# Hybrid retention and attention block: the opening stage of a one-core kernel, divided anew between VectorE and ScalarE

## Chip, cores and metric

One core of a Trainium2 chip runs one launch of the program. The metric is device time in microseconds of that launch, lower is better, given as the median of several runs on the chip.

## What is computed

One encoder layer on 1024 tokens of 1024 features, all in float32. Cut to the part around the change:

```python
mod = jax.nn.silu(c) @ w_ada + b_ada
shift, scale, gate = jnp.split(mod, 3, axis=-1)
h = rms_norm(x, norm_w) * (1.0 + scale[:, None, :]) + shift[:, None, :]
proj = h @ w_in                      # q, k, v, gate columns of retention; latents and gate of attention
...                                  # retention (4 groups of 2 heads), latent attention (8 heads)
y = jnp.concatenate([ret_out, mla_out], axis=-1) @ w_out
x = x + gate[:, None, :] * y
```

Every product `a @ b` is made of three TensorE products of rounded parts (`mm3`, lines 64 to 67): each operand is split into a high part, a cast to fp32r, and a low part, the difference, and high x high, high x low and low x high are summed in PSUM.

## The kernel before

The work is laid out in stages that follow each other on TensorE: the opening; four retention groups with their gates; two gate pieces of the attention; latents; output projection of the retention half; up-projections; attention over eight heads; output projection of the attention half. Features lie on the partitions: `xn` holds the normalised input as eight blocks `k` of 128 features by 1024 tokens, and `hh[k]`, `hl[k]` are the high and the low part of the modulated features.

**The opening** makes `hh` and `hl` and, beside it, the products of the first retention group. Its helpers are:

- `load` (line 134) issues the loads on SyncE's queue: `x` tiles of 128 tokens (512 KB each), rows of `w_ada` for the scale (`s`) and the shift (`b`) of feature block k, and pages `w` of the first group's weights (two feature blocks a page, two buffers).
- `x_tile(t, bank)` (line 148): sum of squares of a token tile on ScalarE, mean on VectorE, the power -1/2 on GpSimd (`r_x`, line 153), the scaling on VectorE or, for the tiles in `XACT`, on ScalarE (lines 155, 157), eight 128x128 transposes on TensorE, and two copies back into `xn` (ScalarE line 164, VectorE line 166).
- `modulation(k)` (line 173): two sums of 1024 products with `silu(c)`; the first on VectorE (line 176), the second on VectorE for k < `KV0` = 2 (line 179) and else as a product on GpSimd (line 182) and a sum on ScalarE (line 183). They give the column pair `b1` (lines 185, 187).
- `features(k, half)` (line 190): scale and shift on VectorE (line 192), the cast to `hh` on ScalarE (194), the difference `hl` on VectorE (195), each for 512 tokens.
- `w_page(j)` (line 200) calls `split`: cast on ScalarE (line 80), difference `wl` on GpSimd (line 81).
- `products(k, lo, hi)` (line 204): three products of 512 columns for each token tile of a half, into eight PSUM banks that stay open over all k: 24 a block, 192 in all.

All eight token tiles are loaded and transposed first, then k runs from 0 to 7 and both halves of the tokens are done for each. The decay masks (24 small GpSimd instructions, lines 269 to 271, with `Exp` on ScalarE) and the rotary tables (VectorE lines 284 to 314, two `Sin` on ScalarE) are made in the same stretch. The opening ends where the first retention gate's product can take a PSUM bank, which the rotary products (lines 352, 354) have to have read: the row of TensorE at 95.81 us.

The program gives the order in which the code issues things, and a scheduler of the framework reorders the instructions within each engine before the run; on the chip every engine then takes its own queue in order, and waits at each instruction for what it needs. `tc.issue_after` keeps the masks behind a named instruction.

Of the kernel before, what the change touches and what calls it, by code (L numbers as in the profile page):

```python
# [30 lines left out]
def body(tc, I, O):  # L31
# [116 lines left out]
    def x_tile(t, bank):  # L148
        """one token tile: its norm, and its features to the partitions"""
        x_ = ld["x", t]  # L150
        i0 = A.activation(xn[:, :, ts_(t)], x_.rearrange("p (a b) -> p a b", b=P), AF.Square, accum_out=msq[:, t:t + 1])
        V.tensor_scalar(out=msq[:, t:t + 1], in0=msq[:, t:t + 1], scalar1=1.0 / D, scalar2=EPS, op0=ALU.mult, op1=ALU.add)
        i1 = G.tensor_tensor(out=r_x[:, t:t + 1], in0=msq[:, t:t + 1], in1=neghalf[:, 0:1], op=ALU.pow)
        if t in XACT:
            A.activation(x_, x_, AF.Copy, scale=r_x[:, t:t + 1])
        else:
            V.tensor_scalar(out=x_, in0=x_, scalar1=r_x[:, t:t + 1], scalar2=None, op0=ALU.mult)
# [9 lines left out]
        return i0, i1  # L167
# [41 lines left out]
    load(*tuple(("x", t) for t in range(8)))  # L209
    nxt = [("s", 0), ("b", 0), ("w", 0), ("s", 1), ("b", 1), ("s", 2), ("b", 2), ("w", 1), ("s", 3), ("b", 3)]  # L210
    nxt = [a for a in nxt if a not in tuple(("x", t) for t in range(8))]
    for t in range(NT):
        x_last = x_tile(t, acc if t % 2 else sm)
        load(nxt.pop(0))
    load(*nxt)
    acc0 += [acc() for _ in range(4)] + [sm() for _ in range(NB0 - 4)]
    for k in range(KT):
        modulation(k)
        if 4 <= k + 3 < KT:
            load(("s", k + 3), ("b", k + 3))  # L220
        if k % 2 == 0:
            w_page(k // 2)
            if 4 <= k + 2 < 8:
                load(("w", k // 2 + 1))
# [739 lines left out]
```

## Time and profile before

| | |
|---|---|
| runs of the kernel before | 1068.68, 1069.62, 1070.6 us (median 1069.62) |
| span of the profiled execution | 1068.5 us (first to last instruction; its time with what lies around the span is not listed apart) |
| busy in the span | TensorE 1020.6, VectorE 592.4, GpSimd 444.0, ScalarE 427.0 us |
| mean granted TensorE clock | 0.986 |
| first 30 us | VectorE 20.08, ScalarE 22.57, GpSimd 13.84, TensorE 17.85 us busy |
| 30 to 60 us | VectorE 30.00, ScalarE 13.55, GpSimd 25.62, TensorE 21.83 us busy |
| 96 us to the end (972.5 us) | TensorE 953.92 us busy |

The span runs from the first to the last instruction. A row of a timeline gives start, duration, engine, line, operation, output <- input, and in brackets how long the engine stood idle before and what ended it. DVE is VectorE, ACT ScalarE, POOL GpSimd, PE TensorE, SP SyncE, PEclk the granted share of TensorE's clock (1 is 2.4 GHz, 0.5 is 1.2 GHz).

### The profile page before, as it was taken

To read this page: it belongs to the slowest core of one execution; us is meant where nothing else is said; L and a number is where in the kernel's file an instruction comes from. 1 tells how busy PE (TensorE), PEld (TensorE's weight loads), DVE (VectorE), ACT (ScalarE), POOL (GpSimd) and SP (SyncE) were. 2 spreads that over 40 slices of the span, in tenths; PEclk is the share of its full clock that TensorE was granted. 3 is DMA by queue.
4 is the path that set the end of the run, shared out by engine and by line. 5 is a ranking of instruction groups with operands and counts; after the bars stand their busy time and mean duration, and the time that the engine had idled before them with its cause. 6 is when DMAs were issued, how large, how long until landed. Compare 5 with 4: busy or idle time off the path is not lost.

```text
span 1068.5 us, 15240 instructions
## 1 busy us (share of the span) xinstructions
PE 1020.6 (96%) x5736; PEld 889.8 (83%) x5736; DVE 592.4 (55%) x1367; ACT 427.0 (40%) x804; POOL 444.0 (42%) x345
## 2 busy tenths in 40 slices
PE   5669999999999999999999999989999999999998
PEld 5457887888888888898888889879999999888887
DVE  6998645544545444335402114867777878874332
ACT  7526312221321322123423005566777776872100
POOL 3877303221421421115534224953465555863210
PEclk8889999999999999999999999999999999999999
DMA  9513101110210201314444730100000000003432
GB/s 373 189 59 113 46 1 60 60 40 21 99 40 21 84 27 62 117 34 177 149 152 147 235 110 21 40 1 1 21 21 2 21 21 21 20 21 118 156 110 69
DMA packets 30744, 82.27 MB, mean 77 GB/s; under 512 B 3536, under 2 KB 4560, under 8 KB 30672
## 3 DMA queue, kind: packets, MB, share of 16 engines
q1 hardware_dynamic: 25920, 72.92, 20.1%
q10 hardware_dynamic: 4752, 8.39, 2.2%
q8 instruction: 45, 0.74, 0.3%
q14 instruction: 27, 0.22, 0.1%
HBM read 64.52 MB, written 16.78 MB: 76 GB/s over the span
## 4 chain that ended last, share of the span: by engine, by line
PE 84%; DVE 10%; DMA 2%; ACT 2%; issue 1%; POOL 1%; ACTq 0%; DVEq 0%; POOLq 0%
PE acc L67 13%; PE acc L66 13%; PE acc L65 13%; PE pt L737 5%; PE sp L65 4%; PE sp L67 4%; PE sp L66 4%; PE po L66 3%; PE po L67 3%; PE po L65 3%; DMA wa<-w_ada 2%; PE sm L66 2%; PE sm L65 2%; PE sm L67 2%; PE sm L423 2%; PE sm L422 2%
## 5 line engine op out<-in xcount | busy, mean ns | idle before, releaser
L81 POOL TENSOR_TENSOR wl<-wr,wh 128x1024 fp32r<-128x1024 f32 (+2 forms) x55 | 124.7, 2275 | 153.0 <-ACT wh L80 139.6
L67 PE MATMUL acc<-wh,hl 128*128 128x512 f32 (+2 forms) x352 | 128.3, 370 | 5.6 <-DVE hl L195 5.5
L65 PE MATMUL acc<-wh,hh 128*128 128x512 f32 (+2 forms) x352 | 128.9, 366 | 1.3 <-ACT xn L164 0.9
L66 PE MATMUL acc<-wl,hh 128*128 128x512 f32 (+2 forms) x352 | 129.3, 367 | 0.0
L723 POOL TENSOR_SCALAR pr<-pr,st 128x1024 f32<-128x1024 f32 x62 | 72.2, 1168 | 100.9 <-DVE st L722 77.6
L740 DVE TENSOR_TENSOR pl<-pt,ph 128x512 fp32r<-128x512 f32 x128 | 85.7, 683 | 31.3 <-ACT ph L739 31.3
L65 PE MATMUL acc<-hh,wh 128*128 128x512 f32 x256 | 101.0, 395 | 1.7 <-DVE t L354 1.7
L66 PE MATMUL acc<-hl,wh 128*128 128x512 f32 x256 | 100.8, 394 | 0.0
L67 PE MATMUL acc<-hh,wl 128*128 128x512 f32 x256 | 100.8, 394 | 0.0
L80 ACT CAST wh<-wr 128x1024 fp32r<-128x1024 f32 (+2 forms) x55 | 53.7, 980 | 106.3 <-PE sm L66 36.7
L739 ACT CAST ph<-pt 128x512 fp32r<-128x512 f32 x128 | 73.3, 590 | 27.4 <-PE pt L737 25.4
L67 PEld LDWEIGHTS acc<-wh,hl 128*128 128x128 f32 x352 | 66.5, 190 | 14.9 <-DVE hl L195 6.7
L721 ACT ACTIVATE pr<-sp,st 128x1024 f32<-128x1024 f32 x62 | 69.6, 1122 | 23.0 <-DVE st L719 22.9
L66 PE MATMUL po<-pl,vh 128*128 128x256 f32 x256 | 76.4, 298 | 2.1 <-DVE pl L740 2.0
L718 DVE TENSOR_REDUCE st<-sp 128x1 f32<-128x1024 f32 x62 | 75.4, 1216 | 4.1 <-PE sp L67 4.0
L65 PEld LDWEIGHTS acc<-wh,hh 128*128 128x128 f32 x352 | 66.3, 188 | 10.7 <-ACT xn L164 1.2
L66 PEld LDWEIGHTS acc<-wl,hh 128*128 128x128 f32 x352 | 66.4, 189 | 9.0 <-POOL wl L81 0.3
L65 PE MATMUL po<-ph,vh 128*128 128x256 f32 x256 | 73.7, 288 | 0.0
L67 PE MATMUL po<-ph,vl 128*128 128x256 f32 x256 | 72.9, 285 | 0.0
L737 PE MATMUL pt<-ident,pr 128*128 128x128 f32 x496 | 69.8, 272 | 2.9 <-DVE st L722 2.7
L358 POOL TENSOR_TENSOR rb<-t,t 128x128 f32<-128x128 f32 x32 | 14.8, 463 | 133.5 <-PE sm L368 66.8
L737 PEld LDWEIGHTS pt<-ident,pr 128*128 128x128 f32 x496 | 57.8, 140 | 7.5 <-issue 2.9
(359 smaller groups left out, 2524.8 us busy)
## 6 DMA issues: line engine op xcount, KB each, us to landing
x<-w_ada SPq DMA_DIRECT2D x16, 512.0 KB, 7.0
wr<-w_ret SPq DMA_DIRECT2D x16, 512.0 KB, 3.5
wr<-w_rg SPq DMA_DIRECT2D x8, 512.0 KB, 3.4
retD<-ro SPq DMA_DIRECT2D x16, 256.0 KB, 2.1
wr<-w_mg SPq DMA_DIRECT2D x8, 512.0 KB, 3.5
wa<-w_ada SPq DMA_DIRECT2D x8, 512.0 KB, 3.5
wr<-w_out SPq DMA_DIRECT2D x8, 512.0 KB, 4.5
wro<-retD SPq DMA_DIRECT2D x8, 512.0 KB, 4.1
```

Source lines behind the costliest of these rows:

```text
L65: T.matmul(out, lh, rh, start=first, stop=False, **kw)
L66: T.matmul(out, lh, rl, start=False, stop=False, **kw)
L67: T.matmul(out, ll, rh, start=False, stop=last, **kw)
L80: A.copy(out=hi, in_=raw)
L81: G.tensor_tensor(out=lo, in0=raw, in1=hi, op=ALU.subtract)
L422: T.matmul(op[:, ts_(h)], sT[t][:, h], vv[t][:, h], start=True, stop=False)
L718: V.tensor_reduce(out=st_[:, 0:1], in_=sp, op=ALU.max, axis=AX.X)
L721: A.activation(pr, sp, AF.Exp, bias=st_[:, 1:2], scale=sc_, accum_out=st_[:, 2:3])
L723: G.tensor_scalar(out=pr, in0=pr, scalar1=st_[:, 3:4], scalar2=0.0, op0=ALU.mult, op1=ALU.add)
L737: T.transpose(tp[:, ts_(q)], pr[:, ts_(half * 4 + q)], ident)
L739: A.copy(out=ph[half][:, :, c_], in_=tv)
L740: V.tensor_tensor(out=pl[half][:, :, c_], in0=tv, in1=ph[half][:, :, c_], op=ALU.subtract)
```

## The change

In the opening, GpSimd keeps `r_x` alone. The second modulation sum of k = 2 to 7 goes from GpSimd and ScalarE to VectorE; the differences `wl` of the first group's four weight pages and the mask terms go from GpSimd to VectorE (three small GpSimd instructions a head become two on VectorE); the scale and shift of the features (16 instructions) goes from VectorE to ScalarE as one `Identity` activation with per-partition scale and bias; two of the eight sums of squares (tiles 3 and 6) go from ScalarE to VectorE, and the three scalings that ScalarE had go to VectorE. The loads are issued for the first four token tiles, then what feature block 0 needs, then the other four tiles; the first half's features and products of block 0 come before tiles 4 to 7. The rotary temporary `rtmp` moves to the ring of weight buffers, and the two `Sin` come behind a named instruction. The pages of later groups are split as before, `wl` on GpSimd.

```diff
-    def split(raw, shape, tag_h="wh", tag_l="wl", pool=None):
+    def split(raw, shape, tag_h="wh", tag_l="wl", pool=None, eng=G):
...
-        G.tensor_tensor(out=lo, in0=raw, in1=hi, op=ALU.subtract)
+        eng.tensor_tensor(out=lo, in0=raw, in1=hi, op=ALU.subtract)
...
-        i0 = A.activation(xn[:, :, ts_(t)], x_.rearrange("p (a b) -> p a b", b=P), AF.Square, accum_out=msq[:, t:t + 1])
+        if t in XDVE:
+            V.scalar_tensor_tensor(out=xn[:, :, ts_(t)], in0=x_.rearrange("p (a b) -> p a b", b=P), scalar=1.0,
+                                   in1=x_.rearrange("p (a b) -> p a b", b=P), op0=ALU.mult, op1=ALU.mult,
+                                   accum_out=msq[:, t:t + 1])
+        else:
+            A.activation(xn[:, :, ts_(t)], x_.rearrange("p (a b) -> p a b", b=P), AF.Square, accum_out=msq[:, t:t + 1])
...
-        if t in XACT:
-            A.activation(x_, x_, AF.Copy, scale=r_x[:, t:t + 1])
-        else:
-            V.tensor_scalar(out=x_, in0=x_, scalar1=r_x[:, t:t + 1], scalar2=None, op0=ALU.mult)
+        V.tensor_scalar(out=x_, in0=x_, scalar1=r_x[:, t:t + 1], scalar2=None, op0=ALU.mult)
...
-        V.scalar_tensor_tensor(out=wa_s, in0=wa_s, scalar=1.0, in1=sc, op0=ALU.mult, op1=ALU.mult,
-                               accum_out=mp[:, 0:1])
-        if k < KV0:
-            V.scalar_tensor_tensor(out=wa_b, in0=wa_b, scalar=1.0, in1=sc, op0=ALU.mult, op1=ALU.mult,
-                                   accum_out=mp[:, 1:2])
-        else:
-            G.tensor_tensor(out=wa_b, in0=wa_b, in1=sc, op=ALU.mult)
-            A.activation(wa_b, wa_b, AF.Copy, accum_out=mp[:, 1:2])
+        for i, kind in enumerate("sb"):
+            wa = ld[kind, k]
+            V.scalar_tensor_tensor(out=wa, in0=wa, scalar=1.0, in1=sc, op0=ALU.mult, op1=ALU.mult,
+                                   accum_out=mp[:, i:i + 1])
...
-        V.tensor_scalar(out=xn[:, k, sl], in0=xn[:, k, sl], scalar1=b1s[k][:, 0:1], scalar2=b1s[k][:, 1:2],
-                        op0=ALU.mult, op1=ALU.add)
+        A.activation(xn[:, k, sl], xn[:, k, sl], AF.Identity, bias=b1s[k][:, 1:2], scale=b1s[k][:, 0:1])
...
-        w0.append(split(ld["w", j], (("p (k n) -> p k n",), {"k": 2})))
+        w0.append(split(ld["w", j], (("p (k n) -> p k n",), {"k": 2}), eng=V))
...
+    rtmp = p_ring.tile([P, 4, NT, 32], F32, name="rtmp", tag="wh")
+    load(*(("x", t) for t in range(4)), ("s", 0), ("b", 0), ("w", 0), *(("x", t) for t in range(4, 8)))
+    for t in range(4):
+        x_tile(t, acc)
+    load(("s", 1), ("b", 1), ("s", 2), ("b", 2))
+    acc0 += [acc() for _ in range(4)]
+    modulation(0)
+    w_page(0)
+    features(0, 0)
+    products(0, 0, 4)
+    for t in range(4, 8):
+        x_tile(t, sm)
+    acc0 += [sm() for _ in range(4)]
     for k in range(KT):
-        modulation(k)
...
+        if k:
+            modulation(k)
...
-        G.tensor_scalar(out=mt, in0=rel[:, 1], scalar1=lg[:, 8 + h:9 + h], scalar2=0.0, op0=ALU.mult, op1=ALU.add)
-        G.tensor_scalar(out=m2, in0=rel[:, 0], scalar1=lg[:, h:h + 1], scalar2=0.0, op0=ALU.mult, op1=ALU.add)
-        G.tensor_tensor(out=mt, in0=mt, in1=m2, op=ALU.add)
+        V.tensor_scalar(out=m2, in0=rel[:, 1], scalar1=lg[:, 8 + h:9 + h], scalar2=None, op0=ALU.mult)
+        V.scalar_tensor_tensor(out=mt, in0=rel[:, 0], scalar=lg[:, h:h + 1], in1=m2, op0=ALU.mult, op1=ALU.add)
...
-XACT, KACT = (3, 5, 7), 1
+XDVE, KACT = (3, 6), 1
```

What the built programs then hold, at three places. First SyncE's queue at the start; `x<-x` and `xl<-x` are token tiles, `x<-w_ada` modulation rows, `wr<-w_ret` weight pages. Before:

```order
L43 DMA small<-small 128x567
L145 DMA x<-x 128x1024 x6
L145 DMA xl<-x 128x1024 x2
L145 DMA x<-w_ada 128x1024 x2
L145 DMA wr<-w_ret 128x1024 x2
L145 DMA x<-w_ada 128x1024 x8
L145 DMA wr<-w_ret 128x1024
L145 DMA x<-w_ada 128x1024 x2
L145 DMA wr<-w_ret 128x1024
L145 DMA x<-w_ada 128x1024 x4
```

In the change:

```order
L43 DMA small<-small 128x567
L145 DMA x<-x 128x1024 x4
L145 DMA x<-w_ada 128x1024 x2
L145 DMA wr<-w_ret 128x1024
L145 DMA x<-x 128x1024 x2
L145 DMA xl<-x 128x1024 x2
L145 DMA wr<-w_ret 128x1024
L145 DMA x<-w_ada 128x1024 x5
L145 DMA wr<-w_ret 128x1024
L145 DMA x<-w_ada 128x1024
L145 DMA wr<-w_ret 128x1024
L145 DMA x<-w_ada 128x1024 x8
```

The modulation rows of feature block 0 and the first weight page moved ahead of the last four token tiles. The third page now comes after five further modulation rows, before after eight; the fourth has eight rows behind it, before four (they follow the part shown).

Second, GpSimd from the `r_x` on (`mt`, `m` are mask terms, `x<-x,sc` the second modulation product). Before, a part:

```order
L153 TENSOR_TENSOR r_x<-msq,neghalf 128x1 x8
L269 TENSOR_SCALAR mt<-small,lg 128x128
L270 TENSOR_SCALAR m_674<-small,lg 128x128
L269 TENSOR_SCALAR mt<-small,lg 128x128
L271 TENSOR_TENSOR mt<-mt,m_674 128x128
L270 TENSOR_SCALAR m_681<-small,lg 128x128
L271 TENSOR_TENSOR mt<-mt,m_681 128x128
L81 TENSOR_TENSOR wl<-wr,wh 128x1024
L270 TENSOR_SCALAR m_688<-small,lg 128x128
L81 TENSOR_TENSOR wl<-wr,wh 128x1024
L182 TENSOR_TENSOR x<-x,sc 128x1024 x2
```

In the change, all up to the first rotary instruction:

```order
L158 TENSOR_TENSOR r_x<-msq,neghalf 128x1 x8
L81 TENSOR_TENSOR wl<-wr,wh 128x1024 x4
L328 MEMSET rb_750 128x512
L328 MEMSET rb_751 128x512
L81 TENSOR_TENSOR wl<-wr,wh 128x1024 x2
```

Only `r_x` and the six differences of later pages (two of the first gate, four of the second group) are left there.

Third, VectorE where the feature blocks 2 and 3 are made (`hl` of blocks 2 and 3, `rtmp` the rotary table, `b` the column pairs). Before:

```order
L176 SCALAR_TENSOR_TENSOR x,mp<-x,sc 128x1024
L288 TENSOR_SCALAR rtmp<-rtmp 128x256
L195 TENSOR_TENSOR hl_94<-xn,hh_86 128x512
L303 COPY rtmp<-rtmp 128x256
L195 TENSOR_TENSOR hl_94<-xn,hh_86 128x512
L185 SCALAR_TENSOR_TENSOR b_518<-mp,small,c_125 128x1
L289 TENSOR_SCALAR rtmp<-rtmp 128x256
L187 TENSOR_TENSOR b_471<-mp,small 128x1
L195 TENSOR_TENSOR hl_95<-xn,hh_87 128x512
L288 TENSOR_SCALAR rtmp<-rtmp 128x256
L195 TENSOR_TENSOR hl_95<-xn,hh_87 128x512
L192 TENSOR_SCALAR xn<-xn,b_471 128x512 x2
```

In the change:

```order
L178 SCALAR_TENSOR_TENSOR x,mp<-x,sc 128x1024
L181 SCALAR_TENSOR_TENSOR b_465<-mp,small,c_125 128x1
L190 TENSOR_TENSOR hl_94<-xn,hh_86 128x512
L178 SCALAR_TENSOR_TENSOR x,mp<-x,sc 128x1024
L190 TENSOR_TENSOR hl_94<-xn,hh_86 128x512
L178 SCALAR_TENSOR_TENSOR x,mp<-x,sc 128x1024
L183 TENSOR_TENSOR b_465<-mp,small 128x1
L270 TENSOR_SCALAR m_687<-small,lg 128x128
L190 TENSOR_TENSOR hl_95<-xn,hh_87 128x512 x2
L181 SCALAR_TENSOR_TENSOR b_511<-mp,small,c_125 128x1
L288 TENSOR_SCALAR rtmp<-rtmp 128x256
L183 TENSOR_TENSOR b_511<-mp,small 128x1
```

The scale-and-shift row (`xn<-xn,b`) is gone from VectorE, and the sums `x,mp<-x,sc` now stand two for each block between the differences.

## Rows read from the trace of the kernel before

**Rows 1.** The page's part 4: the chain of waits, shares of the span by engine.

```profile
PE 84%; DVE 10%; DMA 2%; ACT 2%; issue 1%; POOL 1%; ACTq 0%; DVEq 0%; POOLq 0%
```

**Rows 2.** Windows: start:end, length, busy us (instructions) per engine, PEclk, DMA share, GB/s.

```profile
0.00:30.00 30.00, 17.85 (x88) 15.14 (x89) 20.08 (x64) 22.57 (x39) 13.84 (x23) 0.89 0.94 364
30.00:60.00 30.00, 21.83 (x80) 16.05 (x79) 30.00 (x38) 13.55 (x30) 25.62 (x17) 0.89 0.45 154
...
96.00:1068.50 972.50, 953.92 (x5464) 837.33 (x5463) 509.11 (x1219) 374.60 (x708) 380.99 (x291) 0.99 0.20 66
```

**Rows 3.** Timeline of TensorE: start us, us, instruction, idle before it and its releaser.

```profile
26.23 0.50 PE L65 MATMUL acc<-wh,hh 128*128 128x512 f32 x1 [0.28 <-ACT hh L194]
...
77.61 0.39 PE L65 MATMUL acc<-wh,hh 128*128 128x512 f32 x1
...
80.33 0.39 PE L65 MATMUL sm<-wh,hh 128*128 128x512 f32 x1
...
95.81 0.47 PE L65 MATMUL acc<-hh,wh 128*128 128x512 f32 x1 [1.72 <-DVE t L354]
```

**Rows 4.** Groups of instructions by form, 0 to 96 us, VectorE: busy us, mean ns.

```profile
L195 DVE TENSOR_TENSOR hl<-xn,hh 128x512 fp32r<-128x512 f32 x16 | 21.5, 1350 | 0.4 <-ACT hh L194 0.4
...
L192 DVE TENSOR_SCALAR xn<-xn,b 128x512 f32<-128x512 f32 x16 | 12.8, 832 | 0.0
...
L176 DVE SCALAR_TENSOR_TENSOR x<-x,sc 128x1024 f32<-128x1024 f32 x8 | 12.2, 1522 | 0.0
...
L289 DVE TENSOR_SCALAR rtmp<-rtmp 128x256 f32<-128x256 f32 x3 | 5.1, 1691 | 0.0
...
L288 DVE TENSOR_SCALAR rtmp<-rtmp 128x256 f32<-128x256 f32 x3 | 3.1, 1048 | 0.0
...
L179 DVE SCALAR_TENSOR_TENSOR x<-x,sc 128x1024 f32<-128x1024 f32 x2 | 4.3, 2130 | 0.0
...
L185 DVE SCALAR_TENSOR_TENSOR b<-mp,small,c 128x1 f32<-128x1 f32 x8 | 4.1, 515 | 0.0
...
L157 DVE TENSOR_SCALAR x<-x,r_x 128x1024 f32<-128x1024 f32 x4 | 3.0, 754 | 0.7 <-POOL r_x L153 0.5
```

**Rows 5.** The same view: GpSimd.

```profile
L81 POOL TENSOR_TENSOR wl<-wr,wh 128x1024 fp32r<-128x1024 f32 x9 | 23.8, 2643 | 12.4 <-ACT wh L80 12.4
...
L182 POOL TENSOR_TENSOR x<-x,sc 128x1024 f32<-128x1024 f32 x6 | 16.6, 2770 | 0.0
...
L271 POOL TENSOR_TENSOR mt<-mt,m 128x128 f32<-128x128 f32 x8 | 4.9, 610 | 0.2
```

**Rows 6.** Timeline of VectorE: single instructions, alone or beside GpSimd.

```profile
22.89 0.55 DVE L192 TENSOR_SCALAR xn<-xn,b 128x512 f32<-128x512 f32 x1
...
26.21 2.48 DVE L195 TENSOR_TENSOR hl<-xn,hh 128x512 fp32r<-128x512 f32 x1 [0.42 <-ACT hh L194]
...
28.61 1.21 DVE L176 SCALAR_TENSOR_TENSOR x<-x,sc 128x1024 f32<-128x1024 f32 x1
...
39.27 0.68 DVE L195 TENSOR_TENSOR hl<-xn,hh 128x512 fp32r<-128x512 f32 x1
...
85.58 0.28 DVE L288 TENSOR_SCALAR rtmp<-rtmp 128x256 f32<-128x256 f32 x1
...
93.02 1.99 DVE L274 TENSOR_SCALAR mask<-mask 128x1024 f32<-128x1024 f32 x1 [2.58 <-ACT mask L272]
```

**Rows 7.** Timeline of GpSimd: single instructions.

```profile
9.07 0.56 POOL L153 TENSOR_TENSOR r_x<-msq,neghalf 128x1 f32<-128x1 f32 x1 [1.01 <-DVE msq L152]
...
24.35 0.46 POOL L271 TENSOR_TENSOR mt<-mt,m 128x128 f32<-128x128 f32 x1
...
25.78 2.37 POOL L81 TENSOR_TENSOR wl<-wr,wh 128x1024 fp32r<-128x1024 f32 x1
```

**Rows 8.** Timeline of ScalarE: the nearest rows to the new feature instruction.

```profile
13.40 1.15 ACT L155 ACTIVATE x<-x,r_x 128x1024 f32<-128x1024 f32 x1
...
25.56 0.62 ACT L194 CAST hh<-xn 128x512 fp32r<-128x512 f32 x1
```

More of the change, by code (lines that the diff above doesn't have):

```diff
@@ L150, in x_tile @@
         x_ = ld["x", t]
-        i0 = A.activation(xn[:, :, ts_(t)], x_.rearrange("p (a b) -> p a b", b=P), AF.Square, accum_out=msq[:, t:t + 1])
-        V.tensor_scalar(out=msq[:, t:t + 1], in0=msq[:, t:t + 1], scalar1=1.0 / D, scalar2=EPS, op0=ALU.mult, op1=ALU.add)
-        i1 = G.tensor_tensor(out=r_x[:, t:t + 1], in0=msq[:, t:t + 1], in1=neghalf[:, 0:1], op=ALU.pow)
-        if t in XACT:
-            A.activation(x_, x_, AF.Copy, scale=r_x[:, t:t + 1])
-        else:
-            V.tensor_scalar(out=x_, in0=x_, scalar1=r_x[:, t:t + 1], scalar2=None, op0=ALU.mult)
+        if t in XDVE:
[4 more added lines that the diff above has]
+            A.activation(xn[:, :, ts_(t)], x_.rearrange("p (a b) -> p a b", b=P), AF.Square, accum_out=msq[:, t:t + 1])
+        V.tensor_scalar(out=msq[:, t:t + 1], in0=msq[:, t:t + 1], scalar1=1.0 / D, scalar2=EPS, op0=ALU.mult, op1=ALU.add)
+        G.tensor_tensor(out=r_x[:, t:t + 1], in0=msq[:, t:t + 1], in1=neghalf[:, 0:1], op=ALU.pow)
+        V.tensor_scalar(out=x_, in0=x_, scalar1=r_x[:, t:t + 1], scalar2=None, op0=ALU.mult)
         for z in range(2):
@@ L166, in x_tile @@
                 V.tensor_copy(out=dst, in_=src)
-        return i0, i1
     b1s = {}
@@ L173, in modulation @@
     def modulation(k):
-        wa_s, wa_b = ld["s", k], ld["b", k]
         mp = p_st.tile([P, 2], F32, name="mp", tag="mp", bufs=3)
-        V.scalar_tensor_tensor(out=wa_s, in0=wa_s, scalar=1.0, in1=sc, op0=ALU.mult, op1=ALU.mult,
-                               accum_out=mp[:, 0:1])
-        if k < KV0:
-            V.scalar_tensor_tensor(out=wa_b, in0=wa_b, scalar=1.0, in1=sc, op0=ALU.mult, op1=ALU.mult,
-                                   accum_out=mp[:, 1:2])
-        else:
-            G.tensor_tensor(out=wa_b, in0=wa_b, in1=sc, op=ALU.mult)
-            A.activation(wa_b, wa_b, AF.Copy, accum_out=mp[:, 1:2])
+        for i, kind in enumerate("sb"):
+            wa = ld[kind, k]
+            V.scalar_tensor_tensor(out=wa, in0=wa, scalar=1.0, in1=sc, op0=ALU.mult, op1=ALU.mult,
+                                   accum_out=mp[:, i:i + 1])
         b1 = p_st.tile([P, 2], F32, name="b1", tag="b1", bufs=3)
@@ L207, in products @@
             mm3(acc0[t], hh[k][:, ts_(t)], hl[k][:, ts_(t)], wh[:, k % 2], wl[:, k % 2], k == 0, k == KT - 1)
[L209 to L216, printed above, removed]
-    for k in range(KT):
-        modulation(k)
-        if 4 <= k + 3 < KT:
-            load(("s", k + 3), ("b", k + 3))
-        if k % 2 == 0:
+    rtmp = p_ring.tile([P, 4, NT, 32], F32, name="rtmp", tag="wh")
[11 more added lines that the diff above has]
+    acc0 += [sm() for _ in range(4)]
+    for k in range(KT):
+        if k:
+            modulation(k)
+        if k % 2 == 0 and k + 2 < KT:
+            load(("w", k // 2 + 1))
+        if 3 <= k + 2 < KT:
+            load(("s", k + 2), ("b", k + 2))
+        if k and k % 2 == 0:
             w_page(k // 2)
-            if 4 <= k + 2 < 8:
-                load(("w", k // 2 + 1))
         for half in range(2):
-            i0 = features(k, half)
+            if k or half:
+                i0 = features(k, half)
+                products(k, 4 * half, 4 * half + 4)
             if k == KACT:
-                x_last = i0, x_last[1]
-            products(k, 4 * half, min(4 * half + 4, NB0))
+                x_last = i0
     lg = ctile("lg", 16)
@@ L262, in body @@
     after = ExitStack()
-    for i_ in x_last:
-        after.enter_context(tc.issue_after(i_.ins))
+    after.enter_context(tc.issue_after(x_last.ins))
     for h in range(H):
@@ L280, in body @@
     V.tensor_copy(out=posf, in_=pos_i)
-    rtmp = p_st.tile([P, 4, NT, 32], F32, name="rtmp", tag="xw", bufs=XW)
     ang, nn, nh, yy = (rtmp[:, j] for j in range(4))
@@ L311, in body @@
     V.tensor_scalar(out=yy, in0=yy, scalar1=PI_IN, scalar2=-PI_IN, op0=ALU.min, op1=ALU.max)
+    after = tc.issue_after(x_last.ins)
+    after.__enter__()
     A.activation(Sr, yy, AF.Sin)
@@ L315, in body @@
     A.activation(Cr, nn, AF.Sin)
+    after.__exit__(None, None, None)
     st.close()
@@ L888 @@
 PREP_0 = (2, 4, 5, 6, 6)
-NB0, NACC, XW, KV0 = 8, 4, 8, 2
+NB0, NACC, XW = 8, 4, 8
 WLX = (6, 7)
-XACT, KACT = (3, 5, 7), 1
+XDVE, KACT = (3, 6), 1
 MG0 = 2
```

## Prediction, made before the changed kernel ran

> **What bounds the kernel now.** I read the chain of waits first: 84% of it is TensorE and 10% VectorE [rows 1]. The windows then say where the two lie. From 96 us on TensorE is busy 953.92 of 972.5 us; in the first 60 us it has 17.85 and 21.83 us in windows of 30, while VectorE has no gap at all from 30 to 60 us [rows 2]. So the opening is VectorE's, the rest is TensorE's, and an opening that ends d earlier should end the program d earlier. Its end is one row: the first product of the retention gate, at 95.81 us, after 1.72 us of waiting for VectorE's rotary products [rows 3].
>
> TensorE alone would need far less for the opening: twelve products go by from 77.61 to 80.33 us, 0.227 us each [rows 3], so the 192 are 43.6 us. VectorE is full, but not all with work. The same `hl` difference of 512 columns takes 0.68 us at 39.27 and 2.48 us at 26.21 us [rows 6]; the second stands beside GpSimd's difference from 25.78 to 28.15 us [rows 7] and ends half a microsecond after it. I read that as VectorE waiting for GpSimd to finish and then doing its 0.6 us.
>
> **What VectorE loses to GpSimd.** Busy time of a group less its count times the row that stands alone [rows 4, 6]: `hl` 21.5 - 16 x 0.68 = 10.6; scale and shift 12.8 - 16 x 0.55 = 4.0; first sums 12.2 - 8 x 1.21 = 2.5; second sums 4.3 - 2 x 1.21 = 1.9; the two rotary roundings 5.1 - 3 x 0.28 = 4.3 and 3.1 - 3 x 0.28 = 2.3; column pairs 4.1 - 8 x 0.28 = 1.9; the mask's scaling 1.99 [rows 6] against 0.75 for a scaling of the same width [rows 4], 1.2. Sum **28.7 us**. GpSimd's work in that stretch, at its single rows [rows 7] times the counts: 9 differences and 6 products [rows 5] at 2.37 are 35.6, 24 mask terms at 0.46 (eight each of three kinds; one kind stands in [rows 5]) 11.0, eight `r_x` at 0.56 4.5, together 51.0 us. VectorE loses 0.56 us for each of them.
>
> **The change, part by part.**
> GpSimd keeps the eight `r_x` and, before the first gate product, five differences of later pages: 4.5 + 11.9 = 16.3 us, which at 0.56 cost VectorE 9.2. It gets back 28.7 - 9.2 = **19.5 us**.
>
> VectorE's own list grows. Six second sums at 1.21 are 7.3; four page differences of 1024 columns, of which no row stands alone here, lie between the sum of that width (1.21) and twice the `hl` row (1.36), I take 1.21 as the row of their own width, 4.8; sixteen mask instructions of 128 columns are at most the 0.28 of a 256-wide row, 4.5; two sums of squares 2.4; three scalings at 0.75 2.3; and the 16 scale-and-shift rows leave, -8.8. That is 12.5, and since a record reaches 0.08 us into the next (2.48 from 26.21 ends at 28.69, the next begins at 28.61 [rows 6]), 15 more records are 1.2 us less: **+11.3 us**.
>
> Loads. In the first 30 us VectorE is idle for 9.9 us and the DMA moves 364 GB/s [rows 2], 1.44 us for 512 KB. Block 0's two rows and page come ahead of four token tiles, so 5.8 us sooner, and two sums and a page difference, 3.6 us, can stand in that idle time: **-3.6** (ends 0 and -5.8, no more than the loads come sooner). The four tiles come 3 x 1.44 = 4.3 us later; what hides it is this same work, and TensorE's first twelve products (2.7 us) on the first half. If that cover fails, those 3.6 are gone.
>
> The other pages: the third and the fourth load now wait for VectorE's difference of the first and second page, and behind the fourth on SyncE's queue are eight modulation rows. After the second page's difference VectorE still has five sums, four copies and three differences before it needs a row from behind, over 10 us, against about 3 us for the page and one row. I cost it at nothing; were the cover gone it would be those 3 us. The page differences, now on VectorE, wait for ScalarE's cast; queued behind the first are the scalings of tiles 4 and 5, on which their transposes wait.
>
> ScalarE's feature instruction is a new form. From below a cast of its width bounds it, 0.62, from above a scaled copy of twice its width, 1.15 [rows 8]; I take 0.62, the row of its own width. Sixteen are 9.9 (at most 18.4) us. ScalarE loses three scalings, six sums and two squares, eleven rows of 1024 columns at about 1.15, 12.7 us, and is busy only 13.55 us between 30 and 60 [rows 2]. Nothing on the path. GpSimd's lost time is nothing either; who waited for it was VectorE.
>
> The tail: VectorE's 2.58 us of idle before the mask's scaling [rows 6] go, since the masks are done before the two `Sin` and the table is not loaded again. In their place VectorE waits for ScalarE's cast of a page and a copy behind the cosine, at most 1.15 + 0.62 [rows 8]: **-0.8**.
>
> Sum: 19.5 - 11.3 + 3.6 + 0.8 = 12.6 us. The first gate product comes at 83.2 us, the span is 1068.5 - 12.6 = 1055.9. The median of the runs shown lies 1.1 us over the span of the profiled execution, so I forecast **1057.0 us**. What bears that sum is a row beside GpSimd nearly four times as long as the same row alone [rows 6]. Against this change speaks a sentence of the Trainium skill (Perfetto Trace Analysis, Optimizing Scalar/DVE Operations): with VectorE saturated, it may make sense to move work from it to ScalarE or even GpSimd. Most of this change goes the other way, and by that rule alone nothing would be got back and only the added work would count, some 11 us slower, where the rows give 12.6 us faster.
>
> **The rivals.**
> 1. *GpSimd's rest costs its full length.* The 16.3 us left fall on a VectorE with no gaps, so each stops it for all its length, 16.3 instead of 9.2: gain 5.5, **1064.1 us**. For it: the differences come after the first blocks, where VectorE is densest. Against: GpSimd ran 25.62 of the 30 us window in which VectorE had no gap either [rows 2], and over the stretch VectorE lost 0.56 us for each of its, not one. The Trainium skill (SBUF - State Buffer, Who interferes with whom) has the later of the two fully blocked until the first finishes, which is this case where GpSimd always comes first. 14%.
> 2. *TensorE takes over as the bound.* If the remaining differences are hidden, the opening is first product + products + tail. The first product, now at 26.23 [rows 3], comes at most 5.8 us sooner, 20.4; say 22. 43.6 us at a granted clock of 0.89 [rows 2] are 49.0; 32 transposes of the later tiles at no more than half a product's 0.227 are 3.6, and the two rotary products 1.2 (no wider than 0.6 each): 75.8, a gain of 20.0, **1049.6 us**. It needs nearly all of the 28.7 back. 18%.
> 3. *VectorE's long rows are not GpSimd's doing*, or stay for another reason. Then nothing is got back: the gate comes at 95.8 + 11.3 - 3.6 - 0.8 = 102.7, **1076.5 us**, slower. It decides from the point where VectorE gets back less than 11.3 - 4.4 = 6.9 of the 28.7. Against it: the short rows of the same form in the same stage. 6%.
> 4. *The gain is given back later.* TensorE idles 18.6 us after 96 us [rows 2]; the later pages' differences and loads keep their pace, and if they were late by the whole gain nothing would change, **1069.6 us**. For it only that the code after the opening was scheduled again. 4%.
>
> **How the numbers follow.** My case has 58%. Its own bounds: the page differences 0.6 more, the mask terms 1.8 less, the loads 3.6 less or 2.2 more gain, so 1053 to 1061. The range takes in the first two rivals, 1049.5 to 1064.5, and leaves out what is beyond them and the third and fourth, under 2 in 10. What a measurement can tell from no change is about 0.2%, 2.1 us: faster 0.58 + 0.14 + 0.18 = 0.90, same 0.04, slower 0.06.
>
> **What would show it.** Right: the sixteen `hl` rows fall from a mean of 1350 ns to near 800, the first gate product stands at 83 us, VectorE has no gap from 15 to 75 us, and TensorE after it is as busy as before. Wrong: `hl` rows still over 1.2 us (third rival), TensorE without gaps from 35 us (second), ScalarE's new row over 1.15 us, or a gate product near 83 us and a span that did not follow (fourth).

## The result, and the profile after the change

| | before | after |
|---|---|---|
| median of 4 runs each | 1069.51 us (1068.68 to 1070.6) | 1057.18 us (1057.03 to 1057.49) |
| ratio | | 0.9884, 95% interval 0.987 to 0.9898 |
| span of the profiled execution | 1068.5 us | 1055.3 us (its own time 1057.49) |
| first gate product on TensorE | 95.81 us | 82.51 us |
| first transpose of the first group's output | 170.05 us | 156.48 us |
| first attention product | 713.15 us | 698.41 us |

12.3 us faster; the forecast was 1057.0. Up to the gate 13.3 us are gained, by the attention 14.7, at the end 13.2. The windows of the changed kernel, to be read beside [rows 2]; the first ends at VectorE's first rotary product, the last begins behind the first gate product:

```profile
0.00:81.61 81.61, 64.28 (x272) 52.42 (x272) 73.61 (x169) 51.79 (x92) 24.71 (x22) 0.90 0.61 229
0.00:30.00 30.00, 18.43 (x84) 15.84 (x84) 24.08 (x75) 18.10 (x32) 8.74 (x14) 0.83 0.96 371
30.00:60.00 30.00, 25.02 (x97) 19.69 (x98) 30.00 (x59) 21.07 (x38) 5.93 (x2) 0.89 0.54 200
...
83.00:1055.30 972.30, 953.30 (x5463) 835.43 (x5462) 506.43 (x1219) 372.79 (x704) 377.98 (x290) 1.00 0.20 65
```

The same window of the kernel before ends at its own first rotary product:

```profile
0.00:94.93 94.93, 66.52 (x272) 52.26 (x272) 82.23 (x145) 52.43 (x96) 61.90 (x55) 0.89 0.51 187
```

The third number with a bracket is VectorE: 82.23 us busy and 12.70 idle before, 73.61 and 8.00 after. So 8.6 us of the gain are busy time and 4.7 idle time. Behind the gate TensorE is as busy as it was (953.30 of 972.3 us). The groups of VectorE up to 82.5 us, busy us and mean ns, to be read beside [rows 4]:

```profile
L178 DVE SCALAR_TENSOR_TENSOR x<-x,sc 128x1024 f32<-128x1024 f32 x16 | 21.5, 1347 | 0.0
L190 DVE TENSOR_TENSOR hl<-xn,hh 128x512 fp32r<-128x512 f32 x16 | 12.9, 816 | 0.0
L81 DVE TENSOR_TENSOR wl<-wr,wh 128x1024 fp32r<-128x1024 f32 x4 | 4.8, 1209 | 0.0
...
L270 DVE TENSOR_SCALAR m<-small,lg 128x128 f32<-128x128 f32 x8 | 4.4, 548 | 0.0
```

The `hl` rows fall from 1350 to 816 ns, and the sixteen sums of `L178` take 21.5 us where ten took 16.5. What is left too long stands in single rows of VectorE's timeline (start, duration):

```profile
46.95 2.31 DVE L181 SCALAR_TENSOR_TENSOR b<-mp,small,c 128x1 f32<-128x1 f32 x1
49.18 0.68 DVE L190 TENSOR_TENSOR hl<-xn,hh 128x512 fp32r<-128x512 f32 x1
49.79 3.40 DVE L178 SCALAR_TENSOR_TENSOR x<-x,sc 128x1024 f32<-128x1024 f32 x1
```

and beside them in GpSimd's:

```profile
46.17 5.93 POOL L81 TENSOR_TENSOR wl<-wr,wh 128x1024 fp32r<-128x1024 f32 x2 [18.61 <-ACT wh L80]
```

An instruction on one column, 0.20 us elsewhere, takes 2.31 us and ends where GpSimd's first difference ends (49.25). A sum of 1.21 takes 3.40: the second difference ends at 52.10 and the sum at 53.19, so it does most of its own work behind it. Five such rows stand before the rotary products, one for each difference there, 10.8 us too long together. On TensorE:

```profile
21.79 0.80 PE L65 MATMUL acc<-wh,hh 128*128 128x512 f32 x1 [1.66 <-ACT hh L189]
...
49.92 1.46 PE L67 MATMUL acc<-wh,hl 128*128 128x512 f32 x4 [1.86 <-DVE hl L190]
...
82.51 0.47 PE L65 MATMUL acc<-hh,wh 128*128 128x512 f32 x1 [1.68 <-ACT v L345]
```

Between the last two TensorE has no gap but the 1.68 us at the gate: from 50 us on it is full, and so is VectorE, up to a wait of 1.83 us before its first rotary product.

### The profile page after: what moved, and what is told of

It reads as the page before. It is cut to its first block, busy times and chain, and to the rows that moved or that the text cites. A ratio compares the mean times of both kernels' runs of the same rounds, so it can differ in the third digit from the quotient of the medians.

```text
span 1055.3 us, 15223 instructions
## 1 busy us (share of the span) xinstructions
PE 1018.1 (96%) x5736; PEld 888.3 (84%) x5736; DVE 581.4 (55%) x1390; ACT 426.0 (40%) x800; POOL 404.1 (38%) x311
## 4 chain that ended last, share of the span: by engine, by line
PE 82%; DVE 11%; DMA 2%; ACT 2%; issue 2%; POOL 2%; ACTq 0%; DVEq 0%; POOLq 0%
PE acc L65 13%; PE acc L66 13%; PE acc L67 13%; PE pt L739 4%; PE sp L65 4%; PE sp L66 4%; PE sp L67 4%; PE po L66 3%; PE po L67 3%; PE po L65 3%; DVE x L178 2%; DMA wa<-w_ada 2%; PE sm L425 2%; PE sm L424 1%; PE sm L65 1%
## 5 line engine op out<-in xcount | busy, mean ns | idle before, releaser
L81 POOL TENSOR_TENSOR wl<-wr,wh 128x1024 fp32r<-128x1024 f32 (+2 forms) x51 | 115.2, 2268 | 173.2 <-ACT wh L80 148.9
L723 ACT ACTIVATE pr<-sp,st 128x1024 f32<-128x1024 f32 x62 | 69.5, 1121 | 20.8 <-DVE st L721 20.5
```

The source lines that it names most:

```text
L81: eng.tensor_tensor(out=lo, in0=raw, in1=hi, op=ALU.subtract)
L723: A.activation(pr, sp, AF.Exp, bias=st_[:, 1:2], scale=sc_, accum_out=st_[:, 2:3])
```

## The experiments

All start from the changed kernel but the last. "Rotary" is VectorE's first rotary product, the end of its opening; "gate" is the first gate product on TensorE; "lost" is worked out from VectorE's timeline up to there: every row less the duration of the shortest tenth of its form and width, summed. Each ratio is against runs of the kernel before on the same chip.

| kernel | time us | ratio, 95% interval | rotary | gate | lost |
|---|---|---|---|---|---|
| before | 1069.51 | 1 | 94.93 | 95.81 | 30.9 |
| after | 1057.18 | 0.9884 (0.987 to 0.9898) | 81.61 | 82.51 | 11.9 |
| four_more_differences | 1066.64 | 0.9967 (0.9955 to 0.9978) | 89.35 | 90.25 | 20.5 |
| four_more_memsets | 1059.96 | 0.9912 (0.9896 to 0.9928) | 81.81 | 82.72 | 12.4 |
| four_more_copies | 1058.89 | 0.989 (0.9874 to 0.9907) | 84.08 | 84.98 | 15.2 |
| four_differences_back | 1060.24 | 0.9916 (0.9893 to 0.994) | 84.40 | 85.99 | 18.7 |
| second_sums_back | 1065.13 | 0.9958 (0.9942 to 0.9974) | 88.92 | 92.04 | 21.4 |
| mask_terms_back | 1058.37 | 0.9894 (0.9872 to 0.9917) | 83.25 | 84.86 | 13.8 |
| scale_shift_back | 1067.46 | 0.998 (0.997 to 0.9991) | 89.36 | 90.26 | 12.4 |
| all_tokens_first | 1057.36 | 0.9888 (0.9866 to 0.9909) | 80.49 | 84.39 | 10.7 |
| later_pages_on_vector | 1058.73 | 0.9892 (0.9871 to 0.9913) | 78.01 | 78.91 | 1.5 |
| four_later_pages_on_vector | 1056.10 | 0.9867 (0.9852 to 0.9882) | 76.25 | 77.14 | 3.7 |
| two_gate_pages_on_vector | 1055.05 | 0.9855 (0.984 to 0.9869) | 78.02 | 78.91 | 7.7 |
| long_rows_alone | 1062.38 | 0.9924 (0.9909 to 0.9939) | 89.05 | 89.95 | 14.3 |

### Does GpSimd's work hold VectorE, and which?

My theory: a VectorE row that starts beside a GpSimd difference waits for its end. The rival: the long rows have another cause. Three kernels put four GpSimd instructions at the same places, on rows that are read no more:

```diff
         b1s[k] = b1
+        if 2 <= k <= 5:
+            G.tensor_tensor(out=wa, in0=wa, in1=sc, op=ALU.subtract)
```

In the other two the last line is `G.memset(wa, 0.0)` or `G.tensor_copy(out=wa, in_=sc)`.

Differences.

> The changed kernel with four more GpSimd differences of 1024 columns, on modulation rows of blocks 2 to 5 that have already been summed and are read no more. If a VectorE row that starts beside such a difference waits for its end, as the changed kernel's rows read (2.31 us for a row of 0.2 beside the difference at 46.17 us), each holds VectorE for about 2.2 us in a stretch without gaps: four held rows, first gate product at 82.5 + 8.8 = 91 us, 1066 us. At the 0.56 us per us of the prediction: 4 x 2.37 x 0.56 = 5.3 us, 1062.5 us. If the long VectorE rows are not GpSimd's doing: no long row is added, 1057 us.

Measured: 1066.64 us, gate at 90.25, lost time 8.6 us up, 2.15 for each. GpSimd's row, and VectorE's around it:

```profile
47.64 2.45 POOL L186 TENSOR_TENSOR x<-x,sc 128x1024 f32<-128x1024 f32 x1 [5.80 <-DVE x L178]
```

```profile
47.76 3.42 DVE L178 SCALAR_TENSOR_TENSOR x<-x,sc 128x1024 f32<-128x1024 f32 x1
51.11 0.08 DVE L178 DVE_READ_ACCUMULATOR x<-x,sc 128x1 f32 x1
51.11 0.28 DVE L287 TENSOR_SCALAR rtmp<-rtmp 128x256 f32<-128x256 f32 x1
```

The sum that begins 0.12 us behind it takes 3.42 us in place of 1.21; its neighbour is short again. The theory holds; the rival (no long row added) falls.

Memsets.

> The control: the same four places of the changed kernel, but GpSimd writes zeros there (1024 columns, no operand read; two memsets of half that width take 1.53 us in the changed kernel). If only GpSimd work that reads two SBUF operands holds VectorE: rows as before, first gate product at 82.5 us, 1057 us. If any GpSimd work in SBUF does, at 0.56 us per us: 4 x 1.5 x 0.56 = 3.4 us, 1060.5 us; at its full length 6 us, 1063 us.

Measured: gate at 82.72, lost time 12.4, 0.1 us more for each memset, so nothing worth naming is held. GpSimd writes from 43.72 to 44.67 us, and the sum that begins 0.07 us behind it takes its usual 1.21:

```profile
43.72 0.95 POOL L186 MEMSET x<- 128x1024 f32 x1 [5.95 <-DVE x L178]
```

```profile
43.79 1.21 DVE L178 SCALAR_TENSOR_TENSOR x<-x,sc 128x1024 f32<-128x1024 f32 x1
44.93 0.08 DVE L178 DVE_READ_ACCUMULATOR x<-x,sc 128x1 f32 x1
```

The time, though, was 1059.96 and not 1057. TensorE ended its products sooner here and waited longer for the same gate:

```profile
82.72 0.77 PE L65 MATMUL acc<-hh,wh 128*128 128x512 f32 x1 [3.31 <-ACT v L345]
83.28 0.63 PE L66 MATMUL acc<-hl,wh 128*128 128x512 f32 x1
83.71 0.63 PE L67 MATMUL acc<-hh,wl 128*128 128x512 f32 x1
```

Its products then start 0.43 us apart in place of 0.23, as at 1.2 GHz; the granted clock (the third number from the right) from 82.5 to 92.5 us is 0.69, against 1.00 in the changed kernel, here the second line:

```profile
82.50:92.50 10.00, 9.78 (x33) 7.85 (x34) 7.65 (x21) 4.54 (x12) 6.51 (x8) 0.69 0.29 105
82.50:92.50 10.00, 9.99 (x52) 8.53 (x53) 8.39 (x23) 5.51 (x12) 6.28 (x8) 1.00 0.31 105
```

From the gate to the first output transposes it needs 76.8 us against 74.0: 2.8 us, nearly the whole excess at that point of the profiled execution.

Copies.

> The third of a kind: where the four extra differences and the four memsets stood, GpSimd copies 1024 columns from SBUF to SBUF, one operand read. If it holds VectorE as the differences did: four rows too long by 2 us, gate at 90 us, 1066 us. If it shares with VectorE as the short mask terms did (GpSimd's own row up to three times as long, VectorE's row of 1.21 up to 1.48): 0.3 us for each VectorE row beside it, 1 to 2 us in all, 1058 to 1060 us. If one operand does nothing: as the memsets, gate at 82.7 us.

Measured: gate at 84.98, lost time 15.2, so 0.83 us for each copy of about 1.04:

```profile
45.03 1.11 POOL L186 COPY x<-sc 128x1024 f32<-128x1024 f32 x1 [5.76 <-DVE x L178]
```

```profile
45.16 2.05 DVE L178 SCALAR_TENSOR_TENSOR x<-x,sc 128x1024 f32<-128x1024 f32 x1
```

The sum ends 1.07 us behind the copy's end, so it waited for it and then did its own work: a copy holds VectorE too, for its own length. That is the first case with a shorter row; the time, 1058.89 us, falls where the second had put it. So a row of 1024 columns that reads SBUF on GpSimd holds VectorE, and one that only writes does not. The Trainium skill (SBUF — State Buffer, Who interferes with whom) states just that for a VectorE instruction with two SBUF inputs, and that whoever issues first has the shared pair of ports for its whole instruction; the three kernels agree, with 2.15, 0.83 and about 0.1 us.

### Parts of the change undone

The four page differences back on GpSimd:

```diff
-        w0.append(split(ld["w", j], (("p (k n) -> p k n",), {"k": 2}), eng=V))
+        w0.append(split(ld["w", j], (("p (k n) -> p k n",), {"k": 2})))
```

> The changed kernel with the four page differences of the first retention group back on GpSimd, all else as changed. If each holds VectorE by about 2.2 us in place of 1.21 us of VectorE's own work: 4 us later, first gate product at 86.5 us, 1061.2 us. If GpSimd's differences cost VectorE nothing: 4.8 us sooner, 1052.4 us. At 0.56 us per us the two nearly cancel: 4 x 1.33 - 4.8 = 0.5 us later, 1057.7 us.

Measured: gate at 85.99, 1060.24 us. The first case, within a microsecond; the time alone would not tell it from the changed kernel (its interval begins at 0.9893, the other ends at 0.9898), the gate does.

The second sums back:

```diff
+            if i and k >= 2:
+                G.tensor_tensor(out=wa, in0=wa, in1=sc, op=ALU.mult)
+                A.activation(wa, wa, AF.Copy, accum_out=mp[:, 1:2])
+                continue
             V.scalar_tensor_tensor(out=wa, in0=wa, scalar=1.0, in1=sc, op0=ALU.mult, op1=ALU.mult,
                                    accum_out=mp[:, i:i + 1])
```

> The changed kernel with the second modulation sums of blocks 2 to 7 back as they were: GpSimd's product, ScalarE's sum. VectorE loses six rows of 1.21 us (1.14 each as they overlap, 6.8 us). If a product of GpSimd holds VectorE as the four extra differences did (four held rows, first gate product 7.7 us later), six cost 6 x 2.0 = 12 us: 5 us later, gate at 87.5 us, 1062 us. At 0.56 us per us: 6 x 2.37 x 0.56 = 8.0, so 1.2 us later, 1058.4 us. If products cost VectorE nothing: 1055.5 us, TensorE being without a gap from 50 us on.

Measured: 1065.13 us, 3 more than the dearest case. Lost time rose by 9.5 us, 1.6 a product; what I had left out is that VectorE also waits: it is idle for 12.90 us up to its rotary product, against 8.00 (for masks and features from a fuller ScalarE, 61.8 us busy against 51.8). Two rows show what is held and what isn't, beside GpSimd's

```profile
32.89 2.95 POOL L179 TENSOR_TENSOR x<-x,sc 128x1024 f32<-128x1024 f32 x1 [0.94 <-DMA x<-w_ada]
```

```profile
33.56 0.68 DVE L168 COPY xn<-sm 128x512 f32<-128x512 f32 x1
34.16 1.69 DVE L185 SCALAR_TENSOR_TENSOR b<-mp,small,c 128x1 f32<-128x1 f32 x1
```

The copy from PSUM begins 0.67 us behind the product, lies wholly beside it and takes its usual 0.68; the one-column instruction behind it, on SBUF, takes 1.69 in place of 0.20 and ends with the product, at 35.84.

The mask terms back on GpSimd, with the three removed lines of the change in place of the two new ones.

> The changed kernel with the masks' 24 short instructions of 128 columns back on GpSimd in place of sixteen on VectorE. VectorE loses 8 x 0.27 + 8 x 0.34 less overlap, 3.6 us; GpSimd gets 24 x 0.46 = 11 us. If each holds VectorE for its whole length: 7.4 us later, gate at 90 us, 1064.6 us. At 0.56 us per us, as the prediction had it: 2.6 us later, 1059.8 us. If only long GpSimd rows hold VectorE: no loss, 1055.5 to 1057 us.

Measured: gate at 84.86, 1058.37 us. The middle case at the gate, by another way: VectorE lost only 1.9 us to 11 us of GpSimd, 0.17 for each, and GpSimd's own short rows were stretched instead (from 0.37 to as much as 1.53 us); the rest is VectorE waiting, 10.64 us idle against 8.00.

The scale and shift back on VectorE:

```diff
-        A.activation(xn[:, k, sl], xn[:, k, sl], AF.Identity, bias=b1s[k][:, 1:2], scale=b1s[k][:, 0:1])
+        V.tensor_scalar(out=xn[:, k, sl], in0=xn[:, k, sl], scalar1=b1s[k][:, 0:1], scalar2=b1s[k][:, 1:2],
+                        op0=ALU.mult, op1=ALU.add)
```

> The changed kernel with the sixteen feature scale-and-shift instructions back on VectorE, ScalarE keeping the rest. On VectorE each is 0.55 us less 0.08 of overlap, 7.5 us on an engine without gaps up to the rotary tables: gate at 90 us, 1064.7 us. If TensorE bounds the stretch from 50 us on and VectorE's extra work hides behind it: half of that, 1061 us. If ScalarE's form (0.81 us, not the 0.62 of the prediction) was what set the pace: 1057 us or less.

Measured: gate at 90.26 as in the first case, but 1067.46 us. Behind the gate TensorE waits once for 4.88 us where the changed kernel waits 1.37, at the normalization of the first group's output, and from 180.8 to 184.2 us its granted clock is 0.50 (1.2 GHz), which it isn't in the changed kernel's same stage:

```profile
181.38 0.79 PE L443 MATMUL sm<-ident,o 128*128 128x128 f32 x2 [4.88 <-DVE o L438]
```

The loads and the program with all eight token tiles first:

```diff
-    load(*(("x", t) for t in range(4)), ("s", 0), ("b", 0), ("w", 0), *(("x", t) for t in range(4, 8)))
+    load(*(("x", t) for t in range(8)), ("s", 0), ("b", 0), ("w", 0))
     for t in range(4):
         x_tile(t, acc)
+    for t in range(4, 8):
+        x_tile(t, sm)
...
     products(0, 0, 4)
-    for t in range(4, 8):
-        x_tile(t, sm)
```

> The changed kernel with the loads and the program in the old order: all eight token tiles, then block 0's rows and page, its features and its first products. By the prediction the 3.6 us of work that filled VectorE's idle time in the first 30 us fall behind it again: gate at 86.1 us, 1060.8 us. If the idle time is filled by other work (mask terms, decays) or the gap is covered later: 1057 to 1058 us. If the block comes as late as its transfers do, 5.8 us: 1063 us.

Measured: 1057.36 us, no difference from the changed kernel that can be told. VectorE's first 30 us:

```profile
0.00:30.00 30.00, 18.09 (x84) 16.22 (x85) 24.16 (x74) 19.86 (x35) 5.57 (x14) 0.83 0.96 376
```

It is idle for 5.84 us there, as with the new order (5.92), and its rotary product comes 1.1 us sooner. TensorE pays: its first product is at 28.52 us, not 21.79, and it reaches the gate without a wait, so it is the bound there, 1.9 us later:

```profile
84.16 0.39 PE L67 MATMUL sm<-wh,hl 128*128 128x512 f32 x1
84.39 0.39 PE L65 MATMUL acc<-hh,wh 128*128 128x512 f32 x1
```

### One part alone

On the kernel before, only the six sums and the four page differences on VectorE:

```diff
-        w0.append(split(ld["w", j], (("p (k n) -> p k n",), {"k": 2})))
+        w0.append(split(ld["w", j], (("p (k n) -> p k n",), {"k": 2}), eng=V))
...
-NB0, NACC, XW, KV0 = 8, 4, 8, 2
+NB0, NACC, XW, KV0 = 8, 4, 8, 8
```

> One part of the change alone, on the kernel before: the six second sums and the four page differences of the first group go from GpSimd (and ScalarE) to VectorE; loads, squares, scalings, mask terms and scale-and-shift stay. VectorE's own list grows by 7.3 + 4.8 less overlap, 11.3 us. At the prediction's 0.56 us per us of GpSimd, 23.7 us less GpSimd give back 13.3: 2 us faster than before, 1067.5 us. At 2.0 to 2.2 us for each long row, as the four extra differences cost: 20 to 22 back, 9 to 11 us faster, 1059 to 1061 us. If the scale-and-shift rows, which stay, were the bound: no gain, 1069.5 us.

Measured: 1062.38 us, ratio 0.9924, some 8 us faster than before: two thirds of the gain, a little under the price for each long row and far from the flat 0.56. At the gate it looks different. There only 5.9 of the 13.3 us are gained; VectorE's lost time fell by 16.6 us, 1.7 for each of the ten rows, which lies between the flat price (1.3) and the price of the four extra differences (2.15). The other 2 us came behind the gate, 1.8 of them between the first output transposes (163.92) and the first attention product (705.28). VectorE is still idle for 9.04 us in its first 30.

### GpSimd's last differences moved too

```diff
-        wg = [wpage(I["w_rg"][g][j], 1024, 4) for j in range(2)]
+        wg = [wpage(I["w_rg"][g][j], 1024, 4, eng=V if g == 0 else G) for j in range(2)]
```

This alone is two_gate_pages_on_vector; the other two also take the second group's first two, or all four, pages. All six first.

> The changed kernel with the six page differences of the first gate pages and the second retention group on VectorE too, so that GpSimd has none before the first gate product. VectorE gets back the 10.8 us by which its five held rows are too long and does six rows of 1.21 us, five of them before the gate: 4.8 us. TensorE has no gap from 50 us on; what it can get back is the wait of 1.86 us for an hl row, the half-clock products behind it (8 x 0.2 us) and the 1.68 us before the gate, 5.1 us. So first gate product at 77.5 us, 1052.3 us. If the held rows are not GpSimd's doing: VectorE does 6 us more, 1063 us. If TensorE was already the bound: the last 1.7 us at most, 1055.5 to 1057 us.

Measured: VectorE lost nothing worth naming (1.5 us), TensorE had no gap from 33.6 to 77 us, the gate came at 78.91; but 1058.73 us. 3.6 us ahead at the gate, 2.3 at the first output transposes (156.48 against 154.22), level at the attention (698.41 and 698.48), 1.4 behind at the end. The forecast of the opening was right within 1.4 us and that of the time wrong. Four pages next.

> The changed kernel with four later page differences on VectorE, the two gate pages and the first two of the second retention group; the next ones stay on GpSimd. With six moved, the first gate product came at 78.9 us, 3.6 us sooner, and the time was not better, since VectorE's page differences between the first rotary products, and a wait of 2.1 us for ScalarE's cast of a page at 167 us, gave it back. If what was given back hangs on the last two pages: gate at 79 to 81 us (one hold of 2.1 us at 75 us stays), 1054 to 1055 us. If an earlier opening is given back whatever moves: 1057 to 1059 us.

Measured: gate at 77.14, sooner than the first case had it, and 1056.10 us, between the two cases. Of 5.4 us of lead at the gate 4.0 are left at the first output transposes (152.45) and nothing at the attention (698.36). One place where it is lost is a group of VectorE's rows and what stands beside it on GpSimd, behind the first group's normalization:

```profile
164.47 6.55 DVE L437 TENSOR_SCALAR o<-o,mv,rst 128x128 f32<-128x128 f32 x8 [2.90 <-POOL rst L62]
```

```profile
164.96 2.35 POOL L81 TENSOR_TENSOR wl<-wr,wh 128x1024 fp32r<-128x1024 f32 x1 [0.52 <-ACT wh L80]
...
168.09 2.34 POOL L81 TENSOR_TENSOR wl<-wr,wh 128x1024 fp32r<-128x1024 f32 x1
```

Two differences of the next group fall into eight short scalings on which TensorE's transposes wait; TensorE is busy for 44.97 us from 150 to 200 us, against 47.57 in the changed kernel (second line):

```profile
150.00:200.00 50.00, 44.97 (x237) 37.59 (x236) 26.36 (x76) 13.29 (x23) 16.68 (x17) 0.93 0.19 64
150.00:200.00 50.00, 47.57 (x258) 39.76 (x257) 28.34 (x86) 12.86 (x24) 17.34 (x19) 1.00 0.19 64
```

Part of that busy time is slow as well: behind these waits the granted clock falls to 0.50 (1.2 GHz) from 168.1 to 174.9 us, so it is 0.93 in the window, against 1.00. With six pages moved it is 0.97. Two pages.

> The changed kernel with the two gate pages' differences alone on VectorE. The two held rows at 47 and 50 us (4.3 us too long) go against two rows of 1.21 us: 1.9 us back on VectorE; TensorE's wait of 1.86 us at 49.9 us and the half-clock products behind it (8 x 0.2 us) go too. If VectorE still sets the end through the rotary tables: gate at 80.6 us, 1055.3 us. If the gain is given back behind the gate: 1057 us.

Measured: gate at 78.91, 1.7 us sooner than forecast, and 1055.05 us, ratio 0.9855 (0.984 to 0.9869), the time as forecast. Here the scalings meet one difference and take 4.66 us:

```profile
164.54 4.66 DVE L437 TENSOR_SCALAR o<-o,mv,rst 128x128 f32<-128x128 f32 x8 [2.05 <-POOL rst L62]
```

and TensorE is busy for 47.57 us in that window, at a granted clock of 1.00. It keeps 3.1 of its 3.6 us up to the output transposes and 3.3 to the end of the span (1052.0). Its interval ends just where that of the changed kernel begins (0.987): probably 2 to 3 us better, not shown on one chip side by side. Against the kernel with four pages moved, run on the same chip, its median is 1 us lower, with ranges that just touch.

## Why the prediction was right

| step | forecast | measured |
|---|---|---|
| VectorE gets back from GpSimd | 19.5 us | 19.0 (30.9 less 11.9 lost) |
| VectorE's own list | +11.3 | +10.4 (what is left over: busy 8.6 less, 19.0 got back) |
| idle in the first 30 us | -3.6 | -4.0 (9.92 to 5.92) |
| idle behind it, the tail | -0.8 | -0.7 |
| first gate product | 83.2 us | 82.51 us |
| span | 1055.9 us | 1055.3 us |
| time over the span | 1.1 us | 2.2 us in the profiled execution |

The sum was right within 0.7 us at the gate. That the time agrees within 0.2 us is luck: the span came 0.6 us below the forecast, and the time over the span was taken too small, as the median of several runs less the span of one of them.

- **VectorE held by GpSimd** bore the sum, and the experiments show it. The price did not: 0.56 us per us was a mean over unlike things. On a VectorE without gaps a difference costs 2.15 of its 2.37 us, a copy 0.83 of 1.04, a memset nothing, the short mask terms 0.17 per us. For rows moved, not added, it was 1.6 to 1.7 a row (second_sums_back, four_differences_back, long_rows_alone). What the change left on GpSimd was priced at 9.2 us and lost 11.9 by the rule of the table: five differences cost 10.8, and the eight `r_x` next to nothing. The loss before was put at 28.7 and is 30.9 by the same rule. In the difference, 19.5 against 19.0, the two errors nearly cancelled; for one part alone the flat price missed (2 us forecast; 5.9 measured at the gate, 8 in the time).
- **VectorE's own list** was within a microsecond, though eight of the mask instructions took 0.34 us each where 0.28 was taken for the most.
- **The loads** are the step that failed in its reason. Its 3.6 us came true as 4.0, but with all tokens first VectorE's idle time is the same. Of the 9.9 us, 5.2 lay in the first 8 us, where they are in every kernel; from 8 to 30 us VectorE was idle for 4.7 us before, 0.7 in the change and 0.7 with all tokens first (before, after, all_tokens_first; VectorE is the third number with a bracket):

```profile
8.00:30.00 22.00, 14.10 (x72) 11.66 (x73) 17.28 (x43) 16.95 (x30) 12.64 (x17) 0.84 0.99 392
8.00:30.00 22.00, 14.67 (x68) 12.35 (x68) 21.30 (x55) 12.94 (x25) 7.60 (x8) 0.77 1.03 412
8.00:30.00 22.00, 14.34 (x68) 12.73 (x69) 21.31 (x53) 14.11 (x26) 4.31 (x7) 0.77 1.03 411
```

  As long_rows_alone still has 9.04 us of idle time in its first 30, I take it that the other moved work fills it (squares, scalings, mask terms), which I had costed in full in the list; the squares and scalings were not run by themselves. The mask terms were: with them back on GpSimd it is 6.94 us, and 1.26 of them are one wait for an `r_x` on GpSimd, so a part of it was a wait for GpSimd and no gap to fill. The order itself gives TensorE its start at 21.79 us, 1.9 us at the gate, and no time that can be measured.
- **ScalarE's new instruction** took 0.81 us on the mean, inside its bounds and not the 0.62 I took: 12.2 us for sixteen, with 7.7 us of idle time before them. VectorE never waited for it from 20 to 70 us. Undone, it cost the 7.75 us at the gate that sixteen VectorE rows make.

```profile
L188 ACT ACTIVATE xn<-xn,b 128x512 f32<-128x512 f32 x16 | 12.2, 808 | 7.7 <-DVE b L183 7.7
```

- **SyncE's page loads** cost nothing, as forecast: VectorE is busy for all of 20 to 70 us.
- **First rival** (full length): right for differences (0.9 of their length), wrong for the rest; lost time was 11.9, not 16.3.
- **Second rival** (TensorE the bound): half there. TensorE has no gap from 50 us on, and taking nearly all hold away (lost time 1.5 and 3.7) brought the gate 3.6 to 5.4 us sooner, to 78.91 and 77.14, not to 75.8.
- **Third rival** fell with the four extra differences, and with it the rule weighed against the change: VectorE was saturated, and taking GpSimd's ten long rows onto it was 8 us faster. The Trainium skill (Perfetto Trace Analysis, Optimizing Scalar/DVE Operations) adds that the two share a port, so that moving work between them might not help; this case's runs agree with that half.
- **Fourth rival** (given back later): not here, where 13.3 us at the gate stayed 13.2 at the end. The moves between are small. 1.2 us are gained between the output transposes and the attention; 1.1 of them lie where the kernel before ran at a granted clock of 0.50 from 185.4 to 188.8 us, behind a wait of 1.60 us, and the changed kernel did not. 1.5 are lost behind the attention's first product, of which 0.6 are idle time of TensorE (12.82 us against 12.19); the rest is unexplained. But later waits do answer to the opening: two of the three further moves gave all or most of their gain back there, and scale_shift_back lost 3 us more.

## What to carry to other kernels

Price GpSimd's work by kind before you move it: beside a VectorE without gaps, an instruction of 1024 columns there that reads SBUF cost VectorE most of its own length, one that only writes almost nothing, and short rows (mask terms, `r_x`) little, so a difference of 1024 columns was cheaper on VectorE (1.21 us) than off it (1.6 to 2.2 lost). When two engines are both full, as TensorE and VectorE are here from 50 us on, further relief of one buys only the other's remaining waits, and the next stage's waits, and the clock behind them, must be read before counting it. Undo each part by itself: a term can come true for a reason that isn't the one you gave.

## What was not expected of the hardware

- VectorE's rows that take an operand from PSUM were not held: a copy took 0.68 us beside a GpSimd product, where the next SBUF row waited for the product's end (second_sums_back), and the rotary product at 81.61 us took its usual 0.42, though it began 0.23 us behind a GpSimd difference (after).
- A wait of TensorE can cost more than its length: behind 3.31 us of waiting (four_more_memsets) it ran at a granted clock of 0.69 for ten microseconds, 2.8 us lost by the output transposes, and behind 2.54 us (four_more_differences) at 0.83 from 90 to 100 us. The length of the wait alone does not decide it: behind 2.58 us (four_more_copies) and 1.68 us (after) the clock stayed at 1.00, and behind 1.60 us (before, 183.66) it fell to 0.50 for 3.4 us. What else does, these runs don't show.
- Short GpSimd rows are held in turn: mask terms of 0.37 us took up to 1.53 us beside VectorE's sums (mask_terms_back), and two `r_x` 3.76 us where one alone takes 0.56 (after).
